# Queries and keys scaled straight from PSUM, with a shorter Newton step and a sub-norm without GpSimd

## The chip, the core and the metric

The kernel runs on one core of a Trainium2 chip. The metric is the device time of one execution in microseconds (us), as the median of several runs. The engines are named as in the profile: PE is TensorE (PEld its weight load), DVE VectorE, ACT ScalarE, POOL GpSimd and SP SyncE. Each engine runs its own instructions in one fixed order; an instruction waits on semaphores for the work of others.

## What is computed

A decoder trunk of two layers over 512 tokens with 1024 features, in float32. Layer 0 mixes tokens with differential attention, layer 1 with retention; behind each stand an MLP with a squared ReLU and a gated embedding. The change touches layer 0's attention alone, cut here to what matters:

```python
def rms_norm(x, g):
    y = x * lax.rsqrt(jnp.mean(x * x, axis=-1, keepdims=True) + EPS)      # EPS = 1e-6
    return y * g

def diff_attention(xn, w_qkv, w_o, g_q, g_k, ..., g_sub, lambda_init):    # xn = rms_norm(x, norm_mix)
    qkv = xn @ w_qkv
    q = rms_norm(q, g_q) * (A_DHEAD ** -0.5)     # 8 heads, two halves of 64
    k = rms_norm(k, g_k)
    s = q k^T + bias, causal                     # ALiBi bias
    a = softmax(s)
    attn = a[first half] - lam * a[second half]
    o = attn @ v
    o = rms_norm(o, g_sub) * (1.0 - lambda_init)
    return o @ w_o
```

## The kernel before

Every float32 operand of a matrix product is split into a high part and a low part (`wh`, `wl`, `zh`, `zl`, ...), and one product is three matmuls that add into the same PSUM bank (`mm3`, lines 187 to 189). A block of weights passes through a ring: SP loads it into one of three `raw` buffers, ACT copies it to `wh` (line 74) and writes its negative to `wl` (line 75), and a DMA that POOL issues adds `raw` to `wl` (line 76). A `raw` buffer takes the next block once that DMA has landed; `wh` and `wl` have five buffers each, which come free with PE's last product on them.

Queries and keys come in four groups of two heads, `pqk0` to `pqk3`; a group has four tiles of 128 tokens by 512 columns, each summed over eight blocks of the input, so 24 matmuls a tile. In the profile's names a tile of PSUM shows as `pqk`, its square as `qks`, its scaled form as `qkt`. For each tile:

- `norm_qk` squares it on ACT (`qks`, line 366) and copies it on ACT from PSUM to SBUF with the token's scale `rst` (`qkt`, line 368). DVE sums the squares over the 64 columns of each half head (`qkr`, lines 370 and 371); ACT makes an inverse root of the sum by logarithm and exponential (`qky`, lines 373 and 374); five DVE operations of 128x8 (lines 376 to 380) improve it by a Newton step.
- `scale_qk` multiplies `qkt` on DVE by the result (line 387), in SBUF.
- `turn_qk` transposes it on PE into `ptqk` (line 403) and splits that into `qh`, `ql`, `kh`, `kl` on ACT and DVE (lines 167, 168).

PSUM is handed out in banks by tag: three banks `mm`, two `s` for scores `ps`, two `tr` for transposes (`ptqk`, `pt`, `pn`), one `av` for the product with the values (`po`). The first two tiles of the first group take `s` banks, all other tiles `mm`.

`scores` makes both halves' scores for two heads (line 431), `weigh` adds the bias and takes the minimum on DVE (line 461, `mn`), exponentials on ACT (line 465, `e` and `es`) and the difference on DVE (lines 469 to 473). `turn_a` transposes it, `values` multiplies it with the values into `po`, whose square `osq` goes to `sub_norm`: column sums on PE (`pn`), logarithm, exponential and a square on ACT (lines 503 to 506), then on DVE line 507, on POOL line 508 and on DVE lines 509 and 510, a Newton step and the scale. The output projection (`po__` with a number; line 561 adds it to `x`) uses `mm` banks too.

These functions are called from a list of positions, `plan`, written by hand: products are placed at their count, and scales, transposes and scores some positions behind. From that list a scheduler sets the order of the instructions on each engine.

Of the kernel before, what the change touches and what calls it, by code (L numbers as in the profile page):

```python
# [10 lines left out]
F32 = mybir.dt.float32  # L11
F32R = mybir.dt.float32r
AF = mybir.ActivationFunctionType
ALU = mybir.AluOpType
AX = mybir.AxisListType

P = 128
T = 512
NT = T // P
D = 1024  # L20
# [4 lines left out]
DH = 64  # L25
# [3 lines left out]
EPS = 1e-6  # L29
LAM_INIT = 0.8 - 0.6 * math.exp(-0.3 * 0)  # L30
# [4 lines left out]
C_GQ, C_GK, C_GSUB, C_GGN, C_LAM = 48, 49, 50, 51, 55  # L35
# [65 lines left out]
def decoder_trunk(ctx: ExitStack, tc, xT, pT, small, dist, decay, ident,  # L101
                  w_v, w_qk, w_o, w_up0, w1_0, w2_0, w_g0,
                  w_rv, w_rqk, w_rg, w_ro, w_up1, w1_1, w2_1, w_g1, out):
    nc = tc.nc
# [7 lines left out]
    def ps_mm(name):  # L112
        return psum("mm", 3, name)
# [4 lines left out]
    def ps_tr(name):  # L118
        return psum("tr", 2, name)
# [7 lines left out]
    def slot(name, dt=F32):  # L127
        return gp.tile([P, T], dt, name=name, tag="slot", bufs=SLOTS)
# [56 lines left out]
    def mm3(ps, a, b, start, stop):  # L185

        nc.tensor.matmul(ps, a[0], b[0], start=start, stop=False)  # L187
        nc.tensor.matmul(ps, a[0], b[1], start=False, stop=False)  # L188
        nc.tensor.matmul(ps, a[1], b[0], start=False, stop=stop)  # L189
# [4 lines left out]
    def block(pair, k):  # L194

        return tuple(t.rearrange("p (a n) -> p a n", a=2)[:, k % 2, :] for t in pair)

    def token(pair, tt):
        return cols(pair, slice(tt * P, tt * P + P))
# [59 lines left out]

        return (first, second), rs  # L260

    def rst_columns(acc, rst, name):

        ps = ps_tr(name)
        for tt in range(NT):
            nc.tensor.matmul(ps[:, tt : tt + 1], acc[:, tt * P : tt * P + P], ones[:, 0:1], start=True, stop=True)
        nc.vector.tensor_scalar(
            out=rst, in0=ps[:, 0:NT], scalar1=1.0 / D, scalar2=EPS, op0=ALU.mult, op1=ALU.add
        )
        nc.gpsimd.tensor_tensor(out=rst, in0=rst, in1=mhalf[:, 0:NT], op=ALU.pow)  # L270


    sm = gp.tile([P, N_SMALL], F32, name="sm")
# [7 lines left out]
    mhalf = gp.tile([P, 8], F32, name="mhalf")  # L281
# [7 lines left out]
    acc = slot("acc_a")  # L289
    z = []  # L290
    W.parts = 2
    for k in range(KD):
        t = slot(f"xin{k}")
# [17 lines left out]
    with tc.tile_pool(name="at", bufs=1) as ap:  # L311
        rst = ap.tile([P, NT], F32, name="rst")
# [12 lines left out]
        for k in range(KD):  # L325
            if k % 2 == 0:
                w = W.next()
            for tt in range(NT):
                mm3(pv[tt], token(z[k], tt), block(w, k), k == 0, k == KD - 1)
        rst_columns(acc, rst, "prst0")  # L330
        W.by_dma = True

        idn = ap.tile([P, P], F32, name="idn")
# [17 lines left out]
        nc.vector.tensor_scalar(out=gq, in0=sm[:, C_GQ : C_GQ + 1], scalar1=-(DH ** -0.5), scalar2=None, op0=ALU.mult)  # L351
        gk = sm[:, C_GK : C_GK + 1]
        gs = ap.tile([P, 1], F32, name="gs")
        nc.vector.tensor_scalar(out=gs, in0=sm[:, C_GSUB : C_GSUB + 1], scalar1=1.0 - LAM_INIT, scalar2=None, op0=ALU.mult)

        for tt in range(NT):
            put_v(pv[tt], 0, tt)
# [1 line left out]
        qkt, res, eT, po, oT = {}, {}, {}, {}, {}  # L359
# [3 lines left out]
        def norm_qk(ps, g, tt):  # L363

            sq = slot("qks")
            nc.scalar.activation(out=sq, in_=ps, func=AF.Square, scale=rst[:, tt : tt + 1])
            t = slot("qkt")
            nc.scalar.activation(out=t, in_=ps, func=AF.Copy, scale=rst[:, tt : tt + 1])  # L368
            r = ap.tile([P, 8], F32, name="qkr", tag="qkr", bufs=3)
            nc.vector.tensor_reduce(out=r, in_=sq.rearrange("p (a d) -> p a d", a=8), axis=AX.X, op=ALU.add)  # L370
            nc.vector.tensor_scalar(out=r, in0=r, scalar1=1.0 / DH, scalar2=EPS, op0=ALU.mult, op1=ALU.add)
            y = ap.tile([P, 8], F32, name="qky", tag="qky", bufs=3)
            nc.scalar.activation(out=y, in_=r, func=AF.Ln)
            nc.scalar.activation(out=y, in_=y, func=AF.Exp, scale=-0.5)
            u = ap.tile([P, 8], F32, name="qku", tag="qku", bufs=3)
            nc.vector.tensor_tensor(out=u, in0=y, in1=y, op=ALU.mult)
            nc.vector.tensor_tensor(out=u, in0=u, in1=r, op=ALU.mult)
            nc.vector.tensor_scalar(out=u, in0=u, scalar1=-1.0, scalar2=-0.5, op0=ALU.add, op1=ALU.mult)
            nc.vector.tensor_tensor(out=u, in0=u, in1=y, op=ALU.mult)
            nc.vector.tensor_tensor(out=r, in0=u, in1=y, op=ALU.add)  # L380
            qkt[g, tt] = t, r

        def scale_qk(g, tt):
            t, r = qkt[g, tt]
            a = t.rearrange("p (a d) -> p a d", a=8)
            (
                nc.vector.tensor_tensor(
                    out=a, in0=a, in1=r.rearrange("p (a o) -> p a o", o=1).broadcast_to([P, 8, DH]), op=ALU.mult
                )
            )  # L390

        def turn_qk(g, tt):

# [104 lines left out]
        def sub_norm(h):  # L498
            ps, sq, pair = po.pop(h)
            pn = ps_tr(f"pn{h}")  # L500
            column_sums(pn, pair)

            nc.scalar.activation(out=sq, in_=pn, func=AF.Ln, bias=eps, scale=1.0 / P)
            nc.scalar.activation(out=sq, in_=sq, func=AF.Exp, scale=-0.5)
            u = slot("osu")
            nc.scalar.activation(out=u, in_=sq, func=AF.Square)
            nc.vector.scalar_tensor_tensor(out=u, in0=pn, scalar=P * EPS, in1=u, op0=ALU.add, op1=ALU.mult)
            nc.gpsimd.tensor_scalar(out=u, in0=u, scalar1=-0.5 / P, scalar2=1.5, op0=ALU.mult, op1=ALU.add)
            nc.vector.scalar_tensor_tensor(out=sq, in0=ps, scalar=gs, in1=sq, op0=ALU.mult, op1=ALU.mult)
            nc.vector.tensor_tensor(out=sq, in0=sq, in1=u, op=ALU.mult)  # L510
            oT[h] = slots(f"oT{h}", sq)


# [5 lines left out]
        cur = {}  # L519

        def token_unit(what, b, tt, k):
            if tt == 0 and k == 0:
                cur["blk"] = [W.next() for _ in range(4)]
            if k == 0:
                cur[tt] = (ps_s if (what, b) == ("qk", 0) and tt < 2 else ps_mm)(f"p{what}{b}{tt}")
            mm3(cur[tt], token(z[k], tt), block(cur["blk"][k // 2], k), k == 0, k == KD - 1)
            if k == KD - 1:
                (put_v if what == "v" else norm_qk)(cur[tt], b, tt)
# [3 lines left out]
        for what, b in (("qk", 0), ("qk", 1), ("v", 1), ("qk", 2), ("qk", 3)):  # L532
            if what == "qk":
                qk_at[b] = pos
            for tt in range(NT):
                for k in range(KD):
                    p = tt * KD + k if tt < 2 else 2 * KD + 4 * (k // 2) + 2 * (tt % 2) + k % 2
# [81 lines left out]
        z, acc = zn, st["acc"]  # L619
# [91 lines left out]
    with tc.tile_pool(name="zp", bufs=1) as zp:  # L711
# [9 lines left out]
        z, acc = mlp(z, acc, 0)  # L721
        z, acc = gated_embedding(z, acc, None, 0, False, zslot, made=back)
# [4 lines left out]
        with tc.tile_pool(name="ret", bufs=1) as ap:  # L727
            rst = ap.tile([P, NT], F32, name="rst1")
# [35 lines left out]
            for h in range(RH):  # L764
# [21 lines left out]
                qk = []  # L786
                for n in range(4):
                    w = W.next()
                    ps = ps_mm(f"rqk{h}{n}")
                    for k in range(KD):  # L790
                        mm3(ps, cols(w, slice(k * P, k * P + P)), z[k], k == 0, k == KD - 1)
                    t = ap.tile([P, T], F32, name="rt", tag="rt", bufs=4)
# [21 lines left out]
                for jt in range(NT):  # L814
                    n = T - jt * P
                    ps = ps_s(f"rs{h}{jt}")
# [5 lines left out]
                    t = ap.tile([P, T], F32, name="rt", tag="rt", bufs=4)  # L822
# [5 lines left out]
                for et in range(4):  # L828
                    ps = ps_tr(f"ro{h}{et}")
                    for jt in range(NT):  # L830
                        mm3(ps[:, jt * P : T], cols(v[jt], slice(et * P, et * P + P)), sc[jt], jt == 0, jt == NT - 1)
                    o = slot("ro")
# [30 lines left out]
            for m in range(KD):  # L863
                pu = (ps_tr if m % 2 == 0 else ps_s)(f"pu1{m}")
                up_unit(pu, wu, p1, m)
                t = zslot(f"pus{m}", F32)
                nc.scalar.copy(out=t, in_=pu)
                made.append(t)
            acc = project(RH - 1, go_before)
            z = zn  # L870

        z, acc = mlp(z, acc, 1, late_at=5)
# [84 lines left out]
```

## Time and profile before

| | before |
|---|---|
| median of 3 runs | 1476.94 us (1475.51 to 1478.08) |
| profiled execution, whole | 1477.73 us |
| profiled execution, span from first to last instruction | 1476.0 us |
| PE busy | 1456.2 us, 99% |
| DVE busy | 787.9 us, 53% |
| ACT busy | 648.7 us, 44% |
| POOL busy | 155.2 us, 11% |
| granted TensorE clock, mean | 1.000 |

A row of the profile gives a start and a duration, the engine, the source line, the operation and the tiles written and read. Durations on one engine overlap a little, since an instruction starts before the one ahead of it has wholly ended; where the text speaks of a pitch, it means the distance between starts. `[idle before <-X]` gives the time in which the engine stood still just before, and what ended that. The list of waits adds such times up by what ended them. The granted clock is at its higher level, 2.4 GHz, in the whole span.

### The profile page before, as it was taken

To read this page: it belongs to the slowest core of one execution; us is meant where nothing else is said; L and a number is where in the kernel's file an instruction comes from. 1 tells how busy PE (TensorE), PEld (TensorE's weight loads), DVE (VectorE), ACT (ScalarE), POOL (GpSimd) and SP (SyncE) were. 2 spreads that over 40 slices of the span, in tenths; PEclk is the share of its full clock that TensorE was granted. 3 is DMA by queue.
4 is the path that set the end of the run, shared out by engine and by line. 5 is a ranking of instruction groups with operands and counts; after the bars stand their busy time and mean duration, and the time that the engine had idled before them with its cause. 6 is when DMAs were issued, how large, how long until landed. Compare 5 with 4: busy or idle time off the path is not lost.

```text
span 1476.0 us, 17128 instructions
## 1 busy us (share of the span) xinstructions
PE 1456.2 (99%) x6668; PEld 1195.0 (81%) x6668; DVE 787.9 (53%) x1189; ACT 648.7 (44%) x1007; POOL 155.2 (11%) x127
## 2 busy tenths in 40 slices
PE   9999999999999999999999999999999999999998
PEld 7777667888888888888888888888878888888887
DVE  6776677643434434485464555553684343434455
ACT  6777777742323223354442532433552231323432
POOL 4112112100000000310120200301220000000020
PEclk9999999999999999999999999999999999999999
DMA  6654566853333333244223133142233333333312
GB/s 227 143 115 115 129 170 142 216 158 100 100 90 96 100 101 98 65 152 134 66 88 112 64 101 93 57 129 71 84 102 100 92 94 100 100 98 91 98 58 86
DMA packets 46880, 159.92 MB, mean 108 GB/s; under 512 B 5200, under 2 KB 5712, under 8 KB 46800
## 3 DMA queue, kind: packets, MB, share of 16 engines
q1 hardware_dynamic: 41328, 138.92, 30.1%
q0 software_dynamic: 4896, 17.83, 6.7%
q10 hardware_dynamic: 576, 2.10, 0.4%
q8 instruction: 52, 0.85, 0.2%
q14 instruction: 28, 0.23, 0.0%
HBM read 136.80 MB, written 4.19 MB: 96 GB/s over the span
## 4 chain that ended last, share of the span: by engine, by line
PE 91%; DVE 3%; ACT 2%; DMA 2%; issue 1%; POOL 0%; SPq 0%; ACTq 0%; POOLq 0%; DVEq 0%
PE py L187 8%; PE py L188 8%; PE py L189 8%; PE ph L188 8%; PE ph L187 8%; PE ph L189 8%; PE rg L187 2%; PE rg L188 2%; PE pg L189 2%; PE pg L188 2%; PE pg L187 2%; PE rv L188 2%; PE rqk L188 2%; PE rv L189 2%; PE rqk L189 2%; PE rv L187 2%
## 5 line engine op out<-in xcount | busy, mean ns | idle before, releaser
L83 ACT CAST wh<-raw 128x1024 fp32r<-128x1024 f32 (+1 forms) x211 | 221.0, 1049 | 602.7 <-PE py L188 235.7
L87 DVE TENSOR_TENSOR wl<-raw,wh 128x1024 fp32r<-128x1024 f32 (+1 forms) x211 | 266.8, 1265 | 55.0 <-ACT wh L83 54.0
L188 PE MATMUL ph<-zl,wh 128*128 128x512 f32 x512 | 199.4, 390 | 0.1
L187 PE MATMUL ph<-zh,wh 128*128 128x512 f32 x512 | 199.2, 389 | 0.0
L189 PE MATMUL ph<-zh,wl 128*128 128x512 f32 x512 | 199.2, 389 | 0.0
L187 PE MATMUL py<-hh,wh 128*128 128x512 f32 x512 | 199.2, 389 | 0.0
L188 PE MATMUL py<-hl,wh 128*128 128x512 f32 x512 | 199.2, 389 | 0.0
L189 PE MATMUL py<-hh,wl 128*128 128x512 f32 x512 | 199.2, 389 | 0.0
L654 DVE TENSOR_TENSOR x<-x,py 128x512 f32<-128x512 f32 x64 | 44.0, 688 | 200.0 <-PE py L189 200.0
L644 DVE SCALAR_TENSOR_TENSOR ht<-ph,rsm 128x512 f32<-128x512 f32 x64 | 44.1, 691 | 158.3 <-PE ph L189 158.0
L188 PEld LDWEIGHTS ph<-zl,wh 128*128 128x128 f32 x512 | 96.1, 188 | 20.6 <-DVE zl L168 0.9
L187 PEld LDWEIGHTS ph<-zh,wh 128*128 128x128 f32 x512 | 96.1, 188 | 20.1
L189 PEld LDWEIGHTS py<-hh,wl 128*128 128x128 f32 x512 | 96.1, 188 | 20.1
L189 PEld LDWEIGHTS ph<-zh,wl 128*128 128x128 f32 x512 | 96.1, 188 | 20.0
L187 PEld LDWEIGHTS py<-hh,wh 128*128 128x128 f32 x512 | 96.1, 188 | 20.0
L188 PEld LDWEIGHTS py<-hl,wh 128*128 128x128 f32 x512 | 96.1, 188 | 19.8
L237 POOL TENSOR_TENSOR acc_p<-acc_p,sq 128x512 f32<-128x512 f32 x14 | 24.2, 1726 | 649.0 <-ACT sq L236 649.0
L187 PE MATMUL pqk<-wh,zh 128*128 128x512 f32 x128 | 51.7, 404 | 1.7 <-ACT qkt L368 1.7
L188 PE MATMUL pqk<-wl,zh 128*128 128x512 f32 x128 | 50.9, 398 | 0.8 <-DMA wl<-raw 0.8
L187 PE MATMUL pg<-zh,wh 128*128 128x512 f32 (+1 forms) x136 | 51.2, 377 | 0.0
L189 PE MATMUL pg<-zh,wl 128*128 128x512 f32 (+1 forms) x136 | 51.2, 377 | 0.0
L188 PE MATMUL pg<-zl,wh 128*128 128x512 f32 (+1 forms) x136 | 51.2, 376 | 0.0
(870 smaller groups left out, 2776.8 us busy)
## 6 DMA issues: line engine op xcount, KB each, us to landing
raw<-in_w SPq DMA_DIRECT2D x128, 512.0 KB, 3.6
wl<-raw POOLq DMA_DIRECT2D x34, 512.0 KB, 5.3
raw<-in_w_qk SPq DMA_DIRECT2D x16, 512.0 KB, 3.8
raw<-in_w_g SPq DMA_DIRECT2D x16, 512.0 KB, 3.7
raw<-in_w_rv SPq DMA_DIRECT2D x16, 512.0 KB, 3.7
raw<-in_w_rqk SPq DMA_DIRECT2D x16, 512.0 KB, 4.2
raw<-in_w_rg SPq DMA_DIRECT2D x16, 512.0 KB, 3.6
raw<-in_w_ro SPq DMA_DIRECT2D x16, 512.0 KB, 3.7
```

What stands on the lines that cost most here:

```text
L83: nc.scalar.copy(out=hi[:, s], in_=raw[:, s])
L87: e.tensor_tensor(out=lo[:, r], in0=raw[:, r], in1=hi[:, r].bitcast(F32), op=ALU.subtract)
L187: nc.tensor.matmul(ps, a[0], b[0], start=start, stop=False)
L188: nc.tensor.matmul(ps, a[0], b[1], start=False, stop=False)
L189: nc.tensor.matmul(ps, a[1], b[0], start=False, stop=stop)
L237: (engine or nc.gpsimd).tensor_tensor(out=acc, in0=acc, in1=sq, op=ALU.add)
L644: nc.vector.scalar_tensor_tensor(out=t, in0=s[1], scalar=0.0, in1=rs, op0=ALU.max, op1=ALU.mult)
L654: nc.vector.tensor_tensor(out=x[m], in0=x[m], in1=ps, op=ALU.add)
```

## The change

In layer 0's attention:

- The square no longer carries the token's scale, and the copy `qkt` on ACT is gone. The scale of the token drops out of the normalised value, except in its EPS; a small tile `epsq` of EPS times the token's mean square takes EPS's place (`rst_columns` hands out that mean square, and one DVE operation scales it once).
- `scale_qk` reads the tile in PSUM, multiplies by the inverse root and writes `qkt` in SBUF. So the tile's bank is read last by the scale and not by the copy.
- The Newton step has three DVE operations instead of five.
- `sub_norm` has the Newton factor and the gain `gs` folded together: POOL's operation is gone, DVE has three as before.
- The second tile of the first group takes the `av` bank; before, it took the second `s` bank.

```diff
         nc.vector.tensor_scalar(
-            out=rst, in0=ps[:, 0:NT], scalar1=1.0 / D, scalar2=EPS, op0=ALU.mult, op1=ALU.add
+            out=ms, in0=ps[:, 0:NT], scalar1=1.0 / D, scalar2=EPS, op0=ALU.mult, op1=ALU.add
         )
-        nc.gpsimd.tensor_tensor(out=rst, in0=rst, in1=mhalf[:, 0:NT], op=ALU.pow)
+        nc.gpsimd.tensor_tensor(out=rst, in0=ms, in1=mhalf[:, 0:NT], op=ALU.pow)
...
+        nc.vector.tensor_scalar(out=epsq, in0=epsq, scalar1=EPS, scalar2=None, op0=ALU.mult)
...
-            nc.scalar.activation(out=sq, in_=ps, func=AF.Square, scale=rst[:, tt : tt + 1])
-            t = slot("qkt")
-            nc.scalar.activation(out=t, in_=ps, func=AF.Copy, scale=rst[:, tt : tt + 1])
+            nc.scalar.activation(out=sq, in_=ps, func=AF.Square)
...
-            nc.vector.tensor_scalar(out=r, in0=r, scalar1=1.0 / DH, scalar2=EPS, op0=ALU.mult, op1=ALU.add)
+            nc.vector.tensor_scalar(
+                out=r, in0=r, scalar1=1.0 / DH, scalar2=epsq[:, tt : tt + 1], op0=ALU.mult, op1=ALU.add
+            )
...
-            nc.vector.tensor_tensor(out=u, in0=y, in1=y, op=ALU.mult)
-            nc.vector.tensor_tensor(out=u, in0=u, in1=r, op=ALU.mult)
-            nc.vector.tensor_scalar(out=u, in0=u, scalar1=-1.0, scalar2=-0.5, op0=ALU.add, op1=ALU.mult)
-            nc.vector.tensor_tensor(out=u, in0=u, in1=y, op=ALU.mult)
-            nc.vector.tensor_tensor(out=r, in0=u, in1=y, op=ALU.add)
+            nc.vector.tensor_tensor(out=u, in0=y, in1=r, op=ALU.mult)
+            nc.vector.scalar_tensor_tensor(out=u, in0=u, scalar=-0.5, in1=y, op0=ALU.mult, op1=ALU.mult)
+            nc.vector.scalar_tensor_tensor(out=r, in0=u, scalar=1.5, in1=y, op0=ALU.add, op1=ALU.mult)
+            qkt[g, tt] = ps, r
+
+        def scale_qk(g, tt):
+            ps, r = qkt[g, tt]
+            t = slot("qkt")
+            nc.vector.tensor_tensor(
+                out=t.rearrange("p (a d) -> p a d", a=8), in0=ps.rearrange("p (a d) -> p a d", a=8),
+                in1=r.rearrange("p (a o) -> p a o", o=1).broadcast_to([P, 8, DH]), op=ALU.mult,
+            )
             qkt[g, tt] = t, r
...
-            nc.gpsimd.tensor_scalar(out=u, in0=u, scalar1=-0.5 / P, scalar2=1.5, op0=ALU.mult, op1=ALU.add)
-            nc.vector.scalar_tensor_tensor(out=sq, in0=ps, scalar=gs, in1=sq, op0=ALU.mult, op1=ALU.mult)
-            nc.vector.tensor_tensor(out=sq, in0=sq, in1=u, op=ALU.mult)
+            nc.vector.scalar_tensor_tensor(out=u, in0=u, scalar=-3.0 * P, in1=sq, op0=ALU.add, op1=ALU.mult)
+            nc.vector.scalar_tensor_tensor(out=sq, in0=ps, scalar=gs, in1=u, op0=ALU.mult, op1=ALU.mult)
...
-                cur[tt] = (ps_s if (what, b) == ("qk", 0) and tt < 2 else ps_mm)(f"p{what}{b}{tt}")
+                cur[tt] = ((ps_s, ps_av)[tt] if (what, b) == ("qk", 0) and tt < 2 else ps_mm)(f"p{what}{b}{tt}")
```

The scheduler orders the instructions anew. Line numbers of the changed kernel are 2 to 4 higher here, and the number at the end of a tile's name counts tiles, so that it differs for the same tile.

ACT in the first group, before, from the copy of the second tile (`pqk_435`) to the exponentials of the first scores:

```order
L368 ACTIVATE qkt<-pqk_435,rst 128x512
L167 ACTIVATE qh_455<-ptqk_459,gq 128x2x128
L373 ACTIVATE qky<-qkr 128x8
L374 ACTIVATE qky<-qky 128x8
L167 ACTIVATE kh_457<-ptqk_459,sm 128x2x128
L75 ACTIVATE wl_375<-raw_373 128x1024
L74 CAST wh_374<-raw_373 128x1024
L465 ACTIVATE e_519,su<-e_519,mn 128x128
```

The same place after the change, from the square of the second tile (`pqk_433`):

```order
L370 ACTIVATE qks<-pqk_433 128x512
L75 ACTIVATE wl_384<-raw_382 128x1024
L74 CAST wh_383<-raw_382 128x1024
L377 ACTIVATE qky<-qkr 128x8
L378 ACTIVATE qky<-qky 128x8
L468 ACTIVATE e_514,su<-e_514,mn 128x128
```

The tile's logarithm and exponential, which stood ahead of `kh` and the weight block, now stand behind a weight block's `wl` and `wh`.

ACT between the scores of the first pair of heads, before (`raw_661` is the block on which a later block's load waits):

```order
L465 ACTIVATE e_805,su<-e_805,mn 128x512
L465 ACTIVATE es,su<-es,mn 128x512
L75 ACTIVATE wl_663<-raw_661 128x1024
L74 CAST wh_662<-raw_661 128x1024
L465 ACTIVATE e_822,su<-e_822,mn 128x512
```

The same place after the change (`raw_649` is that block, `e_792` and `e_809` those exponentials):

```order
L468 ACTIVATE e_792,su<-e_792,mn 128x512
L468 ACTIVATE es,su<-es,mn 128x512
L167 ACTIVATE kh_820<-ptqk_822,sm 128x2x128
L468 ACTIVATE e_809,su<-e_809,mn 128x512
L74 CAST wh_650<-raw_649 128x1024
L75 ACTIVATE wl_651<-raw_649 128x1024
```

The block's `wl` has moved behind the second head's exponential and behind its own `wh`.

PE at the change from one query and key block to the next, before: tile 1 of the last group (`pqk_1902`) and the transposes of tile 2 of the third group (`ptqk_1867`):

```order
L188 MATMUL pqk_1902<-wl_1452,zh_3_124 128x512
L189 MATMUL pqk_1902<-wh_1451,zl_3_125 128x512
L187 MATMUL pqk_1902<-wh_1458,zh_4_133 128x512
L188 MATMUL pqk_1902<-wl_1459,zh_4_133 128x512
L189 MATMUL pqk_1902<-wh_1458,zl_4_134 128x512
L403 MATMUL ptqk_1867<-idn,qkt 128x128 x4
```

The same place after the change (tile 1 of the last group is `pqk_1860`, the transposes are `ptqk_1828`):

```order
L188 MATMUL pqk_1810<-wl_1442,zh_7_172 128x512
L189 MATMUL pqk_1810<-wh_1441,zl_7_173 128x512
L406 MATMUL ptqk_1828<-idn,qkt 128x128 x4
L187 MATMUL pqk_1860<-wh_1420,zh_0_84 128x512
L188 MATMUL pqk_1860<-wl_1421,zh_0_84 128x512
```

The transposes, which came after the first fifteen products of the tile, now stand ahead of its first.

## Rows read from the trace of the kernel before

**Rows 1.** Busy time by stretch: stretch, its us, then busy us (count) by engine

```profile
20.00:250.00 230.00, 217.16 (x1115) 165.57 (x1114) 163.97 (x480) 170.90 (x373) 44.84 (x50) 1.00 0.56 138
45.00:65.00 20.00, 19.91 (x108) 15.35 (x108) 14.48 (x56) 17.63 (x42) 3.43 (x4) 1.00 0.79 181
65.00:100.00 35.00, 32.06 (x177) 24.02 (x176) 26.01 (x95) 26.22 (x65) 5.46 (x7) 1.00 0.59 138
150.00:200.00 50.00, 45.24 (x240) 33.45 (x239) 35.35 (x123) 39.34 (x96) 8.25 (x11) 1.00 0.68 159
200.00:250.00 50.00, 46.14 (x225) 34.14 (x225) 37.18 (x87) 35.90 (x71) 10.01 (x11) 1.00 0.51 131
```

**Rows 2.** What PE waited for, 20 to 250 us: us in total, times, longest

```profile
PE ps L431 <- DVE kl L168: 2.1, 2, 1.9
PE pqk L187 <- ACT qkt L368: 1.7, 1, 1.7
PE po L187 <- ACT aT0h L164: 1.4, 1, 1.4
PE ptqk L403 <- DVE qkt L387: 1.4, 2, 0.8
...
PE po__2271 L187 <- ACT qkt L368: 1.0, 1, 1.0
...
PE pn L246 <- POOL osq2l L165: 0.6, 1, 0.6
...
PE ptqk L403 <- DVE qkr L380: 0.4, 1, 0.4
```

**Rows 3.** Groups by shape, 40 to 250 us, of ACT, DVE and POOL: busy us, mean ns

```profile
L368 ACT ACTIVATE qkt<-pqk,rst 128x512 f32<-128x512 f32 x15 | 10.1, 676 | 0.0
L374 ACT ACTIVATE qky<-qky 128x8 f32<-128x8 f32 x15 | 3.1, 208 | 0.2
L387 DVE TENSOR_TENSOR qkt<-qkt,qkr 128x512 f32<-128x512 f32 x16 | 11.0, 689 | 0.3
L378 DVE TENSOR_SCALAR qku<-qku 128x8 f32<-128x8 f32 x15 | 2.5, 170 | 0.3
L561 DVE TENSOR_TENSOR x<-x,po__2245 128x512 f32<-128x512 f32 x1 | 0.7, 681 | 0.0
L508 POOL TENSOR_SCALAR osu<-osu 128x512 f32<-128x512 f32 x7 | 4.3, 618 | 25.2 <-DVE osu L507 25.2
```

**Rows 4.** Chain (start, us), then PE's and DVE's time lines, first scores

```profile
45.39 0.84 PE ps L431 x12
...
46.51 0.40 PE L189 MATMUL pqk<-wh,zl 128*128 128x512 f32 x1
46.74 0.39 PE L187 MATMUL pqk<-wh,zh 128*128 128x512 f32 x1
...
46.39 0.29 DVE L461 CUSTOM_DVE_ANT_0 e<-ps,bias 128x128 f32<-128x128 f32 x1 [0.30 <-PE ps L431]
...
47.24 0.08 DVE L461 DVE_READ_ACCUMULATOR2_ANT mn<- 128x1 f32 x1
```

**Rows 5.** Chain of waits, 74 to 90 us: start, us, what

```profile
76.73 6.31 DMA wl<-raw
...
83.11 5.28 DMA raw<-in_w_qk
...
88.50 1.06 ACT wl L75
...
89.92 0.93 ACT wh L74
```

**Rows 6.** Time lines of ACT and DVE near 165 and 200 us

```profile
165.72 0.67 ACT L368 ACTIVATE qkt<-pqk,rst 128x512 f32<-128x512 f32 x1
...
169.38 0.69 DVE L387 TENSOR_TENSOR qkt<-qkt,qkr 128x512 f32<-128x512 f32 x1
...
200.40 0.67 ACT L368 ACTIVATE qkt<-pqk,rst 128x512 f32<-128x512 f32 x1
```

More of the change, by code (lines that the diff above doesn't have):

```diff
@@ L260, in rs_rows, with rst_columns @@
         return (first, second), rs
-    def rst_columns(acc, rst, name):
+    def rst_columns(acc, rst, name, ms=None):
         ps = ps_tr(name)
@@ L266, in rst_columns @@
             nc.tensor.matmul(ps[:, tt : tt + 1], acc[:, tt * P : tt * P + P], ones[:, 0:1], start=True, stop=True)
+        ms = ms or rst
         nc.vector.tensor_scalar(
-            out=rst, in0=ps[:, 0:NT], scalar1=1.0 / D, scalar2=EPS, op0=ALU.mult, op1=ALU.add
+            out=ms, in0=ps[:, 0:NT], scalar1=1.0 / D, scalar2=EPS, op0=ALU.mult, op1=ALU.add
         )
-        nc.gpsimd.tensor_tensor(out=rst, in0=rst, in1=mhalf[:, 0:NT], op=ALU.pow)
+        nc.gpsimd.tensor_tensor(out=rst, in0=ms, in1=mhalf[:, 0:NT], op=ALU.pow)
     sm = gp.tile([P, N_SMALL], F32, name="sm")
@@ L329, in decoder_trunk @@
                 mm3(pv[tt], token(z[k], tt), block(w, k), k == 0, k == KD - 1)
-        rst_columns(acc, rst, "prst0")
+        epsq = ap.tile([P, NT], F32, name="epsq")
+        rst_columns(acc, rst, "prst0", epsq)
+        nc.vector.tensor_scalar(out=epsq, in0=epsq, scalar1=EPS, scalar2=None, op0=ALU.mult)
         W.by_dma = True
@@ L353, in decoder_trunk @@
         gs = ap.tile([P, 1], F32, name="gs")
-        nc.vector.tensor_scalar(out=gs, in0=sm[:, C_GSUB : C_GSUB + 1], scalar1=1.0 - LAM_INIT, scalar2=None, op0=ALU.mult)
+        nc.vector.tensor_scalar(out=gs, in0=sm[:, C_GSUB : C_GSUB + 1], scalar1=-(1.0 - LAM_INIT) / (2.0 * P), scalar2=None, op0=ALU.mult)
         for tt in range(NT):
@@ L375, in norm_qk @@
             u = ap.tile([P, 8], F32, name="qku", tag="qku", bufs=3)
-            nc.vector.tensor_tensor(out=u, in0=y, in1=y, op=ALU.mult)
-            nc.vector.tensor_tensor(out=u, in0=u, in1=r, op=ALU.mult)
-            nc.vector.tensor_scalar(out=u, in0=u, scalar1=-1.0, scalar2=-0.5, op0=ALU.add, op1=ALU.mult)
-            nc.vector.tensor_tensor(out=u, in0=u, in1=y, op=ALU.mult)
-            nc.vector.tensor_tensor(out=r, in0=u, in1=y, op=ALU.add)
-            qkt[g, tt] = t, r
[L383 to L390, printed above, removed]
+            nc.vector.tensor_tensor(out=u, in0=y, in1=r, op=ALU.mult)
[9 more added lines that the diff above has]
+            )
+            qkt[g, tt] = t, r
         def turn_qk(g, tt):
```

## The prediction

> **What bounds the kernel now.** I read the table of busy time by stretch first. From 20 to 250 us, the attention layer, PE is busy 217.16 of 230.00 us, so it stands still for 12.84 us there; 2.94 of these lie in 65 to 100, 4.76 in 150 to 200 and 3.86 in 200 to 250, while 45 to 65 has only 0.09 [rows 1]. No other engine in that window passes 171 of 230. Everything that the change touches lies in this window, so the most that it could ever win is 12.84 us, 0.87% of the span, and only by ending every one of these waits. There is no such ceiling on a loss. PE has one instruction stream; what it is late at 250 us it is late at the end, because behind that it hardly waits.
>
> The list of what PE waited for then tells which of the waits the edit can reach [rows 2]. Three name things that it removes or shortens: two name ScalarE's copy qkt at L368 (1.7 and 1.0 us: a later tile needs the PSUM bank that the copy reads) and one names the scale at L387 (1.4 us in two waits). The largest, 2.1 us on kl, and the 1.4 us on aT0h aren't named after an edited line.
>
> **The operations themselves.** Removed are 16 copies of 0.676 us on ACT, 16 times two of the small DVE operations (0.17 us each, as L378 shows), and 8 POOL operations of 0.618 us [rows 3]. That is 10.8 us of ACT, 5.4 of DVE and 4.9 of POOL, none of them the bounding engine; the work is worth only what the named waits show. The scale now reads PSUM where it read SBUF. The nearest rows for that: the scale on SBUF took 0.689 us, and an add of the same size that reads PSUM, x<-x,po at L561, took 0.681 [rows 3]. I take no difference.
>
> The Trainium skill ("Perfetto Trace Analysis", section "Optimizing Scalar/DVE Operations") speaks against this edit: it gives a DVE operation about 60 ns of access overhead on SBUF and about 125 ns on PSUM. By it 16 scales would cost some 1.0 us of DVE more, an estimate from that page; the two rows of L387 and L561 show nothing of the kind at this size, and DVE isn't the bound.
>
> **What holds the bank.** Before, a tile's PSUM bank came free when the copy ended, right behind the square. After, it comes free only when the scale has read it: behind square, sum, logarithm, exponential, three small operations and whatever the scheduler has put between them on two engines. That, and the order on ACT, is what I price. The scheduler has reordered much more than the diff says.
>
> **Place 1, about 50 us, first group, second tile.** The second tile now has its own bank, and its products are put behind the first pairs of tiles 2 and 3. On ACT its square is followed by wl and wh of a weight block, and only then by its logarithm and exponential; before, these two weight operations stood behind kh. Counted from the issue of the tile's last product: ACT can start wl when a product three rows on has ended, about 1.1 us (three products at 0.23 us a row and one of 0.39 [rows 4]); wl and wh take 1.06 and 0.93 [rows 5], 1.9 back to back; logarithm and exponential end near 3.4 (0.2 each, L374 [rows 3]); three small DVE operations end at 4.0; then DVE has four reductions of scores in front of the scale, 0.85 us (46.39 to 47.24 in before [rows 4]), and the scale takes 0.69: transposes at about 5.6. PE gets there at about 3.7: 12 products of 0.23 and twelve score products, 0.84 us (the group of twelve [rows 4]). **+1.9 us.** Bounds: nothing, if ACT finds wl's condition fulfilled before the square, and 2.8 if the reductions come as late as the scores allow.
>
> **Place 2, about 62 us, tiles 2 and 3.** In the new order ACT has wl, wh and four exponentials ahead of both squares, and the scores that feed those exponentials come after all products of the two tiles instead of 12 products earlier. From the transposes of place 1: scores at 4.4, exponentials free to run near 6.1 (wl and wh first), four of half the copy's width at an estimated 0.5 each to 8.1, square 8.7, sum 9.3, one attention product and a small operation 9.9, logarithm and exponential 10.3, three small operations 11.0, scale 11.8. PE, with 40 products and twelve score products in between, is there at 10.6. **+1.2 us** (0 to 1.9).
>
> **Scores of the first pair of heads, 65 to 78 us.** Between the pairs of score products there stood 7, 7, 10 and 10 projection products, now 5, 9, 8 and 12. Two gaps lose two products of 0.23 us each, 0.9 us in all, which the other two gaps gain without need. **+0.7** (0 to 1.4).
>
> **Place 3, the ring of weight blocks, 88 us.** PE's longest wait, 1.9 us, is the end of a chain: ACT's wl of one block, its accumulating DMA from 76.73 for 6.31 us, then the raw data of the next block from 83.11 for 5.28 us, then ACT's wl at 88.50, with kh queued behind it [rows 5]. ACT now has an exponential of 128x512 and wh ahead of the wl that starts this chain; the exponential priced like the copy of that size, 0.7, and wh 0.93 make it 1.6 us late, 2.1 if the exponential must wait for its minimum. PE arrives later too, by the 0.7 above. **+1.0** (0.3 to 1.8). Then 98 to 135 us loses two short waits that the edit does shorten, 0.4 on a scale's qkr and 0.6 on POOL [rows 2]: **-1.0** (-1.2 to 0).
>
> **Place 4, about 165 us, third group.** Before, the first product of tile 1 of the next block waits 1.7 us [rows 2] for tile 2's copy (165.72 to 166.39 [rows 6]), does fifteen products and only then comes to the transposes of that tile, with the scale at 169.38 [rows 6]. Now the transposes stand directly in front of that product, and both need the scale. Without copies on the way: second square 165.7 to 166.3, logarithm and exponential to 166.7, then on DVE the second sum, one attention product and three small operations, scale from 168.4 to 169.1. PE, there at 164.7 as before (1.7 ahead of the copy's end), waits 4.4 instead of 1.7; the block it waits for a little earlier may give 0.7 of that back. **+2.0** (0.5 to 2.7).
>
> **184 to 188 us.** 13 products now lie before the product on aT0h and the copies have gone from ACT ahead of it: the 1.4 us [rows 2] go, but I leave a third of it to the next wait on its path. **-0.9** (-1.9 to 0).
>
> **Place 5, about 200 us, fourth group.** Before, 1.0 us on the copy (200.40 to 201.07 [rows 6]), then 0.8 on the scale [rows 2]. Now the output projection's bank waits for tile 2's scale, and ACT has a second square (from 200.4, where the copy stood, 0.6), a weight block's wh (0.93), the logarithm (0.2), another square (0.5) and the exponential (0.2) in its chain, then DVE three small operations (0.6) and the scale (0.69): it ends near 204.1. PE, there at 200.1, waits 4.0 instead of 1.8; some of the second wait will come back. **+2.0** (-0.5 to 3). From 215 to 250, where after 201 to 206 some 2 us of the stretch's 3.86 remain [rows 1], the shorter sub-norm and ACT without copies help: **-0.8** (-1.9 to 0).
>
> Sum: 1.9 + 1.2 + 0.7 + 1.0 - 1.0 + 2.0 - 0.9 + 2.0 - 0.8 = +6.1 us. The profiled execution took 1477.73 us (span 1476.0 and 1.7 around it), so 1483.8 by it; it lies 0.8 us above the median of the three runs, 1476.94, so 1483 for a median. The terms' bounds are wide, but they hang together in one direction: a PE that is late gives the ring time. For this case alone 1479.9 to 1488.
>
> **Rivals.** A: the edit does what it removes. Two waits on copies (2.7), the waits on the scale (1.4), POOL (0.6) and part of aT0h (0.9) go, and the chains at places 1 and 2 find enough cover: -5.6 at most, likely -4 to -5, time about 1472. For it: these waits stand by name in the list [rows 2]. Against it: the bank is not free any sooner, the order on ACT is worse in four places. It decides if place 1 and place 2 show no wait on the scale. B: exchange. Place 4 and 5 cost as much as the other waits give, places 1 to 3 about 1 us each: between -2 and +2.9, about 1478. For it: the ring has its own pace, and PE that is late at 65 us finds blocks that have landed, so that +3 there would eat the 1.9 at 88 us. C, the forecast, ends on the slower side: the bank held until the scale, and weight copies in the chain of the norm; it decides from the point at which places 1, 4 and 5 together exceed 3.5 us more than what goes.
>
> **How the numbers follow.** A measurement here tells 0.2%, about 3 us, from no change. C 0.60, B 0.24, A 0.16. The range leaves out a tenth on either side: low within A, 1471.5; high 1488.5, which is C with most terms at the upper bound. Faster 0.16, same 0.24, slower 0.60.
>
> **What would show it.** In the trace of after: 45 to 65 us with about 3 us of idle PE instead of 0.09; a wait of PE on the scale (the new L389) near 51, 63, 166 to 169 and 201 to 205, in total 8 us or more; the wait on ps near 92 longer than 1.9; PE's sums in 150 to 250 lower by about 2 us. The forecast is wrong if the first two transposes of the group run without a wait, or if ACT has wl done before the square, or if the ring's lateness is swallowed. A DVE scale much longer than 0.69 us would show the price from PSUM that I set at nothing.

## The result, and the profile after

The changed kernel took 1488.97 us (median of 4 runs, 1487.31 to 1489.89) against 1476.22 us before: a ratio of 1.0084, 95% interval 1.0067 to 1.0102. So it is slower, as forecast, but by 12.75 us where 6.1 were forecast, and above the upper end of the range, 1488.5. Four more runs later gave 1486.06 us and a ratio of 1.0060 (1.0044 to 1.0077), about 9.7 us. The two rounds differ by 2.9 us, so the size of the loss is known only to lie near 10 to 13 us. One execution of the kernel with six idle matmuls below took 2436.89 us at a mean clock of 0.556; it stands apart from all others and is left out of the median there.

| | before | after |
|---|---|---|
| profiled execution, whole | 1477.73 us | 1487.31 us |
| its span | 1476.0 us | 1485.3 us |
| DVE busy | 787.9 us | 784.7 us |
| ACT busy | 648.7 us | 639.4 us |
| granted TensorE clock, mean of the span | 1.000 | 0.997 |

Busy time by stretch in the kernel after, with the columns of [rows 1]; the third figure from the end is the granted clock, which is 1.00 in every row of [rows 1]:

```profile
20.00:250.00 230.00, 211.80 (x1081) 162.09 (x1080) 156.15 (x443) 154.10 (x346) 36.91 (x40) 0.98 0.53 132
45.00:65.00 20.00, 17.41 (x97) 13.57 (x96) 12.93 (x50) 14.61 (x37) 2.55 (x3) 1.00 0.82 188
65.00:100.00 35.00, 32.42 (x178) 24.07 (x176) 25.83 (x89) 24.09 (x62) 4.69 (x6) 1.00 0.50 117
150.00:200.00 50.00, 43.34 (x215) 32.38 (x213) 32.54 (x104) 34.54 (x81) 7.72 (x10) 0.93 0.50 118
200.00:250.00 50.00, 44.64 (x228) 33.62 (x228) 35.05 (x89) 31.09 (x69) 5.21 (x5) 0.97 0.53 146
...
250.00:300.00 50.00, 48.81 (x212) 39.17 (x212) 32.15 (x45) 39.66 (x59) 10.39 (x11) 1.00 0.79 199
```

PE stands still for 18.20 us in 20 to 250 us, where it was 12.84, and for 1.19 us in the next 50, where it was none: 6.55 us more. But the span grew by 9.3 us. The difference, 2.8 us, has its place in the clock column: 0.93 and 0.97 in the two stretches that had 1.00.

What PE waited for in the kernel after, 20 to 270 us (us in total, times, longest), beside [rows 2]:

```profile
PE ptqk L406 <- DVE qku L381: 5.7, 3, 4.3
PE po__2220 L187 <- DVE qkt L389: 3.6, 1, 3.6
PE ptqk L406 <- DVE su L472: 3.5, 2, 2.0
PE po L188 <- DVE aT0l L165: 1.5, 1, 1.5
PE po__2760 L187 <- ACT oT6h L164: 1.0, 1, 1.0
```

The waits on ACT's copy are gone, and so is most of the one on kl. In their place stand waits of the transposes `ptqk` and of the output projection on the scale. Where the list names `qku` or `su`, that is the short DVE instruction directly behind the scale, which ends within 0.1 us of it; the transposes read what the scale writes.

The stretch around the longest of them, PE's time line in the kernel after, and behind it the row of the scale, which ends at 170.63:

```profile
165.83 0.40 PE L188 MATMUL pqk<-wl,zh 128*128 128x512 f32 x1
166.07 0.39 PE L189 MATMUL pqk<-wh,zl 128*128 128x512 f32 x1
170.78 1.09 PE L406 MATMUL ptqk<-idn,qkt 128*128 128x128 f32 x4 [4.32 <-DVE qku L381]
171.51 0.78 PE L187 MATMUL pqk<-wh,zh 128*128 128x512 f32 x1
172.09 0.63 PE L188 MATMUL pqk<-wl,zh 128*128 128x512 f32 x1
172.51 0.63 PE L189 MATMUL pqk<-wh,zl 128*128 128x512 f32 x1
...
174.59 0.40 PE L189 MATMUL pqk<-wh,zl 128*128 128x512 f32 x1
174.83 0.40 PE L187 MATMUL pqk<-wh,zh 128*128 128x512 f32 x1
...
169.94 0.69 DVE L389 TENSOR_TENSOR qkt<-pqk,qkr 128x512 f32<-128x512 f32 x1
```

Ahead of the wait two products start 0.24 us apart; behind it 0.42 to 0.43, until about 174.6, then 0.24 again. It is the lower of TensorE's two levels, 1.2 instead of 2.4 GHz, as the granted clock of two windows says, each one at the end of one of the two long waits and behind it:

```profile
171.00:173.00 2.00, 2.00 (x8) 1.71 (x8) 1.97 (x5) 0.48 (x1) 0.00 (x0) 0.50 0.60 152
...
209.00:211.00 2.00, 1.74 (x5) 1.38 (x6) 1.11 (x4) 0.00 (x0) 0.75 (x1) 0.50 1.02 369
```

Behind the first wait five products lose some 0.2 us each and two groups of four transposes about 0.35 each, 1.7 us; behind the second it is about 1.2. Together 2.9, near the 2.8 that the waits leave over.

The granted clock of 1.000 for the kernel before, which stands ahead of the prediction for the whole span, does not hold for its start. There the first products start 0.43 us apart, as they do behind the long waits, until about 10.4 us; from 10.7 us on it is 0.23:

```profile
8.66 0.63 PE L188 MATMUL pv<-wl,zh 128*128 128x512 f32 x1
9.08 0.63 PE L189 MATMUL pv<-wh,zl 128*128 128x512 f32 x1
```

The profile gives 1.00 for 5 to 10 us all the same, so the mean clock does not count this. The profiled execution of the changed kernel started in the same way (until 10.7 us), so the comparison of the two is not disturbed; that of the second round did not (0.23 us from 6.3 us on), and its first query and key product comes at 29.09 us instead of 30.80. That is 1.7 of the 2.9 us between the rounds, in these two executions; how the others started is not known.

### The profile page after: what moved, and what is told of

It is laid out like the page before. It is cut to its first block, busy times and chain, and to the rows that moved or that the text cites. A ratio compares the mean times of both kernels' runs of the same rounds, so it can differ in the third digit from the quotient of the medians.

```text
span 1485.3 us, 17077 instructions
## 1 busy us (share of the span) xinstructions
PE 1459.1 (98%) x6668; PEld 1197.6 (81%) x6668; DVE 784.7 (53%) x1158; ACT 639.4 (43%) x991; POOL 150.7 (10%) x119
## 4 chain that ended last, share of the span: by engine, by line
PE 88%; DVE 4%; issue 4%; ACT 2%; DMA 1%; POOL 0%; SPq 0%; POOLq 0%; ACTq 0%; DVEq 0%
PE py L187 8%; PE py L189 8%; PE py L188 8%; PE ph L187 8%; PE ph L188 8%; PE ph L189 8%; PE rg L187 2%; PE rg L188 2%; PE pg L189 2%; PE pg L188 2%; PE pg L187 2%; PE rv L188 2%; PE rqk L188 2%; PE rv L187 2%; PE rv L189 2%
```

## The experiments

Theory 1 of the expectations is that PE waits on the scale because the bank is held until then, and that the clock falls behind those waits. The rivals are that the new order of the engines costs by itself, and that the clock falls on its own account.

**The copy restored in the third and fourth group.**

```diff
             nc.scalar.activation(out=sq, in_=ps, func=AF.Square)
+            t = ps
+            if g >= 2:
+                t = slot("qkt")
+                nc.scalar.copy(out=t, in_=ps)
...
-            qkt[g, tt] = ps, r
+            qkt[g, tt] = t, r
...
-            t = slot("qkt")
+            t = ps if g >= 2 else slot("qkt")
```

> The changed kernel with ScalarE's copy from PSUM restored in the third and fourth group of queries and keys (16 tiles, 8 copied); the first two groups scale from PSUM, and everything else stays as changed. Theory 1 (the loss behind 150 us is the bank that is held until the scale, and the clock that falls after the two long waits it makes): PE's waits near 166 us (4.3 us) and 206 us (3.6 us) shrink to 2 us or less each, the granted clock stays at 1.00 in every stretch, and the time goes from about 1489 to 1480 to 1483 us; the two waits near 51 and 63 us stay (1.5 and 1.0 us). Rival (the new order of ACT and PE makes these waits, or the clock falls on its own account): both long waits or the low clock remain, time 1486 to 1490 us.

Measured: 1481.53 us (10 runs), 1.0031 times before (1.0017 to 1.0044), so of the loss 4.5 us (against the second round of the changed kernel) to 7.4 us (against the first) go. Of what PE waited for, 20 to 250 us:

```profile
PE ptqk L410 <- DVE su L476: 3.5, 2, 2.0
PE po L187 <- ACT aT0h L164: 1.5, 1, 1.5
...
PE pqk L187 <- ACT qkt L374: 1.4, 1, 1.4
...
PE po__2229 L187 <- ACT qkt L374: 0.6, 1, 0.6
```

The two long waits became 1.4 and 0.6 us on the copy, as the theory said. The clock did not stay at its upper level, as had been expected: three windows of this kernel, behind a wait of 2.0 us at 84.7, one of 1.5 at 188.3 and one of 1.4 at 227.7 (with a short one of 0.8 behind it), show

```profile
88.00:90.00 2.00, 2.00 (x7) 1.51 (x6) 1.34 (x5) 1.42 (x6) 0.02 (x1) 0.50 1.11 268
...
190.00:192.00 2.00, 2.00 (x5) 1.61 (x6) 1.90 (x14) 0.80 (x4) 0.00 (x0) 0.50 1.19 197
...
231.00:233.00 2.00, 2.00 (x7) 1.47 (x6) 1.52 (x3) 0.78 (x1) 0.88 (x1) 0.50 0.00 0
```

So a fall also comes behind shorter waits, in one execution and not in another: the profiled execution of before has waits of 1.9, 1.7 and 1.4 us [rows 2] and none.

**The copy restored in the first and second group.** The condition is `g < 2`.

> The changed kernel with ScalarE's copy restored in the first and second group; the third and fourth scale from PSUM, and on PE the transposes of the third group's tile 2 still stand ahead of the next block's tile 1. Theory 1: the long waits near 165 us (4 us or more) and 205 us (3 us or more) stay, each with a stretch at clock 0.50 behind it; the waits before 100 us sum to about 2.5 us as in the kernel before instead of 5; 1484 to 1487.5 us. Rival (the clock falls by chance and not by those waits): no low clock near 170 and 209 us, 1479 to 1482 us.

Measured: 1488.47 us (4 runs), 1.0081 (1.0066 to 1.0096). What PE waited for, and a window of two microseconds behind either long wait:

```profile
PE ptqk L410 <- DVE qku L385: 4.0, 1, 4.0
PE po__2228 L187 <- DVE qkt L393: 3.6, 1, 3.6
```

```profile
172.00:174.00 2.00, 1.88 (x7) 1.71 (x8) 1.90 (x6) 0.62 (x2) 0.00 (x0) 0.50 0.57 219
212.00:214.00 2.00, 2.00 (x9) 1.65 (x8) 0.23 (x1) 0.47 (x1) 0.00 (x0) 0.60 0.66 248
```

The long waits and the falls behind them stay, as the theory said; a third fall comes at a wait of 1.9 us near 50 us. The time was missed: it lies 0.5 us below the first round of the changed kernel and 2.4 above the second, so nothing was won. Up to 100 us PE's waits shrink to 2.9 us, but between 127 and 147 us four new ones, twice on POOL's split of `osq`, on the sub-norm and on a scale, add 2.1 us. The waits of the first two groups are exchanged.

**The copy restored in all four groups.** What is left of the change is the second tile's bank, the EPS by token, the Newton step and the sub-norm.

> The changed kernel with the copy restored in all four groups: the second tile's bank, the shorter Newton step and the sub-norm without GpSimd are left. Theory 1: no wait over 2 us, 1475.5 to 1479 us, the same as the kernel before within what can be told. Rival (the reordering of the small edits costs by itself): 1480 us or more.

Measured: 1480.89 us (10 runs), 1.0028 (1.0017 to 1.0040): above theory 1 and in the range of the rival. The trace of the profiled execution, the fastest of the ten (1477.55 us), has no more idle time of PE than before; the runs differ by their mean clock. Those at 0.999 took 1477.55, 1478.34 and 1479.10 us, those at 0.996 took 1481.28 to 1482.23. The work and its order are the same in all of them, so the clock is worth about 1.2 us here for 0.001 of the mean. That is not a fixed price: a straight line through the runs of the kernel before gives 1.5 to 1.9 us for 0.001 in three sets of 19 to 31 runs, and leaves over a third of their spread to something else. The mean clock of these ten runs is 0.9970, against 0.9985 for the kernel before in the same rounds; at 1.2 that is about 2 of the 4.5 us lost.

**The copy everywhere, and the second tile in its first bank.** As the last, with the choice of banks as before the change.

> The changed kernel with the copy restored for all 16 tiles and the second tile back in the scores' bank: what is left of the change is the shorter Newton step, the EPS by token and the sub-norm without GpSimd. Theory 1: these cost nothing and give back at most the short wait on POOL (0.6 us) and a little in 180 to 250 us: 1474.5 to 1477.5 us, clock 1.00, no wait over 2.5 us. Rival (any edit reorders the engines and that alone costs): 1480 us or more.

Measured: 1478.74 us (10 runs), 1.0015 (0.9999 to 1.0030). The interval ends at no change; a gain is not to be seen, and the time lies above the expectation. The longest waits are 1.6 us or less, as expected, but the clock isn't 1.00: the profiled execution (1481.49 us, above the median) is at 0.50 behind three of them. Whether the small edits cost 2 us or nothing is left open.

**The second tile's bank alone**, in the kernel before:

```diff
-                cur[tt] = (ps_s if (what, b) == ("qk", 0) and tt < 2 else ps_mm)(f"p{what}{b}{tt}")
+                cur[tt] = ((ps_s, ps_av)[tt] if (what, b) == ("qk", 0) and tt < 2 else ps_mm)(f"p{what}{b}{tt}")
```

> The kernel before with one line changed: the second tile of the first group in the values' bank. Theory 1 (the bank's move puts the second tile's products later and two weight operations of ACT ahead of its logarithm, which is what costs in 45 to 65 us, also with the copy): PE stands still for 2 to 3.5 us in 45 to 65 us instead of 0.09, time 1478 to 1480.5 us. Rival (the move costs only together with the scale from PSUM): under 0.7 us there, 1476 to 1477.5 us.

Measured: 1476.87 us (10 runs), 0.9996 (0.9983 to 1.0009), no change. Theory 1 was wrong here: in 45 to 65 us PE stands still for 1.48 us, a wait of 1.3 at 49.9 us on the scale, but the two waits of the kernel before at 84 and 88 us, 2.4 us together, shrink to 0.4. What the first group loses comes back at the ring of weight blocks: over 20 to 250 us PE stands still for 12.78 us, where it was 12.84. The time is the rival's, the idle time in the first group neither's.

The opposite, scaling from PSUM with the second tile in the scores' bank, wasn't tried: as the list of positions stands, both banks for scores would then be held by tiles that are still to be scaled.

**The long wait filled.** In the changed kernel, ahead of the transposes of the third group's tile 2:

```diff
             pt = ps_tr(f"ptqk{g}{tt}")
+            if (g, tt) == (2, 2):
+                for _ in range(14):
+                    nc.tensor.matmul(pt, z[0][0][:, 0:P], z[0][0], start=True, stop=True)
```

> The changed kernel with 14 idle matmuls of 128x512 put directly ahead of the transposes that wait 4.3 us near 166 us; their results are overwritten. PE then does 3.2 us of work in the wait and stands still for about 1.1. Nothing that the wait depends on is moved. Theory 1 (the clock falls because PE stands still for over 3.5 us): the granted clock stays 1.00 from 165 to 180 us, the matmuls behind the wait start every 0.23 us instead of 0.43, and the time falls by 1.5 to 2 us, more if later places gain; the fall near 209 us may remain. Rival (the clock falls from something else at that point, for instance what the other engines or the DMAs draw): still 0.5 in 171 to 175 us, time the same or up to 1 us longer.

Measured: 1480.53 us (10 runs), 1.0026 (1.0014 to 1.0038), 5.5 to 8.4 us below the two rounds of the changed kernel, far more than expected. PE's time line there, the granted clock, and PE's busy time over the layer and the 50 us behind it:

```profile
163.19 0.39 PE L189 MATMUL pqk<-wh,zl 128*128 128x512 f32 x1
163.42 3.36 PE L397 MATMUL ptqk<-zh 128*128 128x512 f32 x14
166.61 0.39 PE L187 MATMUL pqk<-wh,zh 128*128 128x512 f32 x1
...
168.51 0.66 PE L412 MATMUL ptqk<-idn,qkt 128*128 128x128 f32 x4 [0.16 <-DVE qkt L389]
168.93 0.47 PE L188 MATMUL pqk<-wl,zh 128*128 128x512 f32 x1
169.24 0.39 PE L189 MATMUL pqk<-wh,zl 128*128 128x512 f32 x1
169.47 0.39 PE L187 MATMUL pqk<-wh,zh 128*128 128x512 f32 x1
```

```profile
170.00:175.00 5.00, 5.00 (x29) 3.35 (x28) 3.89 (x15) 3.43 (x10) 0.00 (x0) 1.00 0.35 106
...
20.00:300.00 280.00, 267.99 (x1339) 207.71 (x1338) 190.55 (x490) 197.51 (x408) 48.22 (x52) 1.00 0.60 150
```

The scheduler put the 14 matmuls seven products ahead of the transposes. PE hardly stands still, the clock is 1.00 in the whole stretch, and products start every 0.23 us. That is what theory 1 says of the clock. The rest of the gain is the order: behind this point the scheduler has arranged the engines anew, and the second long wait, 3.6 us in the changed kernel, is 0.6 us here. The two profiled executions, which started alike, tell the parts apart: in 20 to 300 us PE stands still for 12.0 us instead of 19.4, and 3.2 of these 7.4 are filled, so 4.2 are the order; the spans differ by 7.5, which leaves about 3.3 for the clock.

This run shows one thing more. The bank is held until the scale in all four groups here, as in the changed kernel, and the time is about that of the kernel with copies in the third and fourth group. At the place of the second long wait the scale ends no earlier, 4.9 us behind the start of the tiles' squares (4.6 in the changed kernel), but PE comes to the product that needs the bank 4.3 us behind them instead of 1.1. So holding the bank costs what it did only in an order in which PE has little else to do ahead of it; to that extent the rival of the order is right.

**The changed kernel again.**

> The changed kernel once more, unaltered. Theory 1 (waits of PE, and TensorE's clock that falls behind them): the waits near 51, 63, 85, 166 and 206 us come back with 1.5, 1.0, 2.0, 4.3 and 3.6 us within 0.3; the granted clock falls to 0.50 behind the two long ones, and where a run shows a mean clock of 0.995 or less there is a third stretch at 0.50 behind one of the waits of 1.5 to 2 us. 1487 to 1490 us. Rival (the earlier figure was an outlier of one chip): 1480 to 1485 us.

Measured: 1486.06 us (4 runs), 1.0060 (1.0044 to 1.0077), a little below the expected 1487. The waits come back to 0.1 us (1.55, 1.05, 1.99, 4.33 and 3.58), so the program makes them in both executions. The mean clocks of the runs were 0.995, 0.996, 0.996 and 0.998, the last for the fastest, 1482.96 us; in the first round they were 0.997 for 1487.31 and 0.995 for the other three. The third stretch that was expected in a run at 0.995 isn't there: the second of the two lasted longer. A window of this execution, behind the wait of 3.6 us, which ended at 207.55:

```profile
210.00:212.00 2.00, 2.00 (x7) 1.52 (x6) 1.44 (x3) 0.95 (x2) 0.00 (x0) 0.50 0.28 109
```

**Shorter waits filled in the kernel before.** The same lines with six matmuls, in the kernel before, where the waits near 163 us are 0.75 and 1.7 us:

> The kernel before with six idle matmuls of 128x512 (1.4 us of PE) ahead of its waits near 162 to 166 us, which are 0.75 and 1.7 us; their results are overwritten. Theory 1 (the clock also falls behind waits of 1.5 to 2 us, in some executions, and that is part of the kernel's time and spread): the two waits shrink by 1.4 us together, no stretch at 0.50 within 165 to 175 us, and the time is 0 to 2 us below that of the kernel before, 1474.5 to 1477 us. Rival (falls come at any place): the time rises by up to 1.5 us.

Measured: 1474.62 us (9 runs), 0.9989 (0.9979 to 0.9999). In its trace neither wait is left, and the clock is 1.00 from 165 to 175 us. Once more, with more runs:

> The kernel before with the six idle matmuls near 163 us once more, to see whether it is faster than the kernel before. Theory 1: 1474 to 1476 us, 0.5 to 2.5 us below the kernel before of the same rounds, mean clock of its runs 0.998 to 1.000. Rival (the first figure was chance): within 0.3 us of it.

Measured: 1474.54 us (12 runs), 0.9990 (0.9977 to 1.0003): the same gain, with an interval that just takes in no change. Its profiled execution (1477.14 us, above the median) shows that the same program doesn't always wait alike: PE waits 1.13 us near 166 us and again near 170, where the first trace has nothing. The clock falls behind a wait of 2.0 us on kl at 87.6:

```profile
92.00:94.00 2.00, 2.00 (x7) 1.61 (x7) 1.89 (x8) 2.00 (x8) 0.00 (x0) 0.50 0.98 152
```

**And that wait filled too**, with six matmuls more ahead of the transposes `pt` of the first head's second block:

```diff
             pt = ps_tr(f"pt{h}{kt}")
+            if (h, kt) == (0, 1):
+                fill(pt, 6)
```

> As the last, with six more idle matmuls ahead of the transposes near 87 us, before the wait on kl of 1.6 to 1.9 us. That wait ends with a load of weights, which the matmuls don't move. Theory 1: the wait shrinks to under 0.6 us and nothing else moves, so no PE time is won but one place less behind which the clock can fall: 1473.5 to 1476 us, the same as the last within what can be told. Rival (the matmuls delay the transposes and what hangs on them): 1476 us or more.

Measured: 1473.39 us (12 runs, 1472.50 to 1474.41), 0.9978 (0.9968 to 0.9988). Its median is below that of both kernels, with more work on the bounding engine. PE's time line at the added matmuls, and the whole attention layer:

```profile
86.93 1.52 PE L394 MATMUL pt<-zh 128*128 128x512 f32 x6
88.29 0.49 PE L490 MATMUL pt<-idn,e 128*128 128x128 f32 x3
89.36 0.39 PE L437 MATMUL ps<-kl,qh 64*128 64x256 f32 x2 [0.58 <-DVE kl L168]
```

```profile
20.00:250.00 230.00, 224.01 (x1143) 171.44 (x1142) 167.94 (x486) 175.29 (x378) 46.66 (x52) 1.00 0.57 143
```

The wait on kl is 0.58 us instead of 1.9, by 1.4 us of idle work. The runs' mean clock is 0.9998, against 0.9983 for the kernel before in the same rounds; at 1.2 us for 0.001 that is 1.8 of the 2.6 us, at the kernel before's own 1.9 all of it. The spread shrank with it: 1.9 us from the fastest to the slowest of 12 runs, 7.8 in 23 runs of the kernel before. The fastest run of the kernel before (1471.86) is faster than any of these twelve: what the filling took away is the upper end. In the profiled executions the new order behind the first six matmuls also shortens waits (PE stands still for 5.99 us in the layer, and 2.7 are filled, of 12.84 in [rows 1]); what each of the two is worth over all runs wasn't separated.

## Why the prediction was wrong

**The sum of the waits was right, in part by luck; the time of the work between them was not.** The terms against the idle time of PE at the same places in the two traces:

| place | forecast, us | measured, us |
|---|---|---|
| 1, near 51 us | +1.9 | +1.5 |
| 2, near 63 us | +1.2 | +1.0 |
| scores, 65 to 78 us | +0.7 | 0.0 |
| 3, the ring, 84 to 93 us | +1.0 | 0.0 |
| 98 to 135 us | -1.0 | -0.6 |
| 155 us, no term | 0 | -0.2 |
| 4, 162 to 171 us | +2.0 | +2.4 |
| 184 to 193 us | -0.9 | -0.2 |
| 5, 200 to 209 us | +2.0 | +1.7 |
| behind 215 us | -0.8 | +1.0 |
| sum | +6.1 | +6.6 |

Places 1, 2, 4 and 5 came out within 0.4 us, by the chains that were given. The other terms missed by 0.4 to 1.8 us each, and that the sum still fits is luck: 1.7 us of loss at the scores and the ring did not come, while the stretches from 98, from 184 and behind 215 us came out 2.9 us worse than forecast. For place 1 the rows of ACT and DVE after read like the working:

```profile
47.04 0.59 ACT L370 ACTIVATE qks<-pqk 128x512 f32<-128x512 f32 x1
47.73 1.06 ACT L75 ACTIVATE wl<-raw 128x1024 fp32r<-128x1024 f32 x1
48.69 1.03 ACT L74 CAST wh<-raw 128x1024 fp32r<-128x1024 f32 x1
49.63 0.20 ACT L377 ACTIVATE qky<-qkr 128x8 f32<-128x8 f32 x1
49.86 0.21 ACT L378 ACTIVATE qky<-qky 128x8 f32<-128x8 f32 x1
...
50.50 0.17 DVE L383 SCALAR_TENSOR_TENSOR qkr<-qku,qky 128x8 f32<-128x8 f32 x1
...
51.48 0.69 DVE L389 TENSOR_TENSOR qkt<-pqk,qkr 128x512 f32<-128x512 f32 x1
```

Square, weight block, logarithm, exponential, Newton, four score reductions, scale; the transposes follow at 52.3, 1.55 us after PE was ready.

**The step that failed is the one from the waits to the time, "Sum: ... so 1483.8 by it"**: it adds waits to before's time and so takes PE's work between them at before's pace. It has no term for the clock behind the waits and gives no reason for leaving it out. Behind the waits of 4.3 and 3.6 us the clock is at its lower level for some microseconds, which costs 2.9 us in the profiled execution. Over all its runs the changed kernel had a mean clock of 0.9955 and 0.9962 in the two rounds, the kernel before 0.998 to 0.9985; 0.0025 at 1.2 us for 0.001 is 3 us. Waits of 6.6 and 3 us of clock make 9.6: the second round's difference, and three short of the first's. For 1.7 of these three the profiled executions show the slower start told of above, but in the first round the kernel before started so as well where it was profiled; the cause of the three stays open. The granted clock of 1.000 came from one profiled execution of the kernel before; its other runs had mean clocks from 0.996 to 1.000.

**Two small terms had the wrong place.** The scores' shorter gaps cost nothing. At the ring, the wait did not grow on kl; 0.5 us is left of it, and a wait of 2.0 us on the scale at 85.5 us stands ahead of it instead, so PE comes to the scores later. The prediction had named this, the ring's lateness swallowed, as a sign of being wrong. The wait of 1.0 us on `oT6h` at 261 us is new and wasn't foreseen; it is most of the largest miss, behind 215 us.

**What the change's parts cost** comes from four kernels: copies in groups 3 and 4 back, 4.5 to 7.4 us won, 7.6 where groups 1 and 2 have their copies too; copies in groups 1 and 2 back, between 0.5 us won and 2.4 lost; the second tile's bank alone, nothing that can be told. With all copies back 2 to 4.5 us of loss remain, which no run puts down to one of the small edits; that the new order costs them is not ruled out. So the larger part of the loss lies where the bank was held for the next block's tile and for the output projection, places 4 and 5, in the order that the scheduler made: the run with the long wait filled won as much with the banks still held. Places 1 and 2 were read rightly, but what is lost there the kernel with copies loses elsewhere, the exchange of rival B.

**Rival A** (the named waits go) was half true: the two waits on the copy (1.7 and 1.0 us) went, and larger ones on the scale came. The 1.4 us on aT0h, of which two thirds were to go, came back as 1.5 on aT0l. **Price of PSUM as source**: the scale's row after,

```profile
L389 DVE TENSOR_TENSOR qkt<-pqk,qkr 128x512 f32<-128x512 f32 x16 | 11.0, 686 | 0.2
```

is 0.686 us against 0.689 from SBUF [rows 3], so the value taken, nothing, holds, and the access overhead that the Trainium skill ("Perfetto Trace Analysis", section "Optimizing Scalar/DVE Operations") puts higher for PSUM does not show at this shape. ACT's square takes 0.582 us against 0.677 in the trace of before, without the scale operand now; no step had counted that.

## What to carry to other kernels

Scaling straight from PSUM saves a copy and keeps the bank until the whole chain of a norm has run; count who waits for that bank, and how much other work stands ahead of that in its engine's order, before counting the copy. Where PE is the bound, a wait has two prices, the time itself and the slower work behind it: read the granted clock of several executions, not of one, and look at the pace of the products too. Here a few long waits were dearer than many short ones. Idle matmuls in two waits did not lengthen this kernel; with the order that came of them they lowered its median by 0.2%.

## What the runs showed of the hardware

The clock of TensorE falls to its lower level (granted 0.50, products every 0.42 us instead of 0.23) for some microseconds in or behind waits of PE. At the six waits of 3.6 us and more in the three profiled executions that have them it fell every time; in the wait of 4.3 us of the kernel after it was at 0.50 from 168 us on, while PE still stood still. At waits of 1.3 to 2.0 us it fell in some and not in others, 11 of 32 in the twelve profiled executions (of the kernel before with six idle matmuls, one fell behind the wait on kl and one did not). Every stretch at the lower level inside the attention layer had such a wait ahead of it, and where the wait was filled with idle matmuls, none came. Over the runs of the kernel before, the mean clock goes with somewhat over half of the spread in time.

At the start of the program the first products ran 0.43 us apart until about 10.5 us in three profiled executions (before, after, and the long wait filled) and not in the others, while the profile gives a granted clock of 1.00 there.
